# Expert weights of a routed layer loaded in 8 KB runs per partition, and the product that brings slots back to tokens taken one column half after the other

## The chip, the core and the metric

The kernel runs on one core of one Trainium2 chip. The metric is the time of one execution on the device in microseconds (us); lower is better. The core has a matrix engine (PE, with its weight loads listed as PEld), three engines for elementwise work (DVE, ACT, POOL), a queue engine (SP) that only issues transfers here, and 16 DMA engines that move the data.

## The reference, cut to what matters

256 tokens of width 1024 pass through a first block (a gated recurrence, an attention with differences, then a layer of 32 experts) and through a second block of two layers. All numbers are 32-bit. The part that the change touches is the layer of experts:

```python
x = x + hier_moe(h2, w_rg, b_rg, w_re, b_re, w_eg, w_eu, w_ed)
# each token goes to 2 of the 32 experts (one of 4 groups, two of the 8 experts in it);
# expert e on a token h of width 1024:
#   y = (silu(h @ w_eg[e]) * (h @ w_eu[e])) @ w_ed[e]
# w_eg[e], w_eu[e]: [1024, 512]; w_ed[e]: [512, 1024]; the two y are weighted by the router's gates
```

The 96 matrices are 2 MB each, 201 MB in all, and each is read once.

## The kernel before, in words

Every weight of the kernel is read from HBM as a *chunk* of 1 MB, in the order in which PE will want it. `add` (L161) enters a chunk in that list, and `pump` (L175) issues its DMA on the SP queue as soon as one of the buffers is free. SP takes the list strictly in order. A buffer comes free through `drop` when the matmuls that read it have run. During the layer of experts there is more room than elsewhere: `raw` (3 buffers) and `rawB` (4) hold a chunk each; up to four more chunks lie in the pairs `wh` and `wl` (half a chunk in each of the two, so two DMAs of 512 KB), one lies in the two `gain` tiles (two DMAs again), and single tiles that nothing else needs then (`XH`, `hT`, at the start also `XL`, `S2`/`S`, `xg`, `w`) hold one each. That makes about 14 MB.

`moe_chunks` (L1120) enters 192 chunks: for each pair of experts, first four for `w_eg`, four for `w_eu`, then four for `w_ed` (an expert's matrix is two chunks, `hf` 0 and 1). A chunk of `w_eg` or `w_eu` is a tile of 128 partitions x 4 x 512: partition p holds the rows hf * 512 + k * 128 + p for k = 0 to 3, which are 4 separate pieces of 2 KB in HBM. A chunk of `w_ed` is 128 x 2 x 1024, two pieces of 4 KB on each partition.

`moe` (L1136) first splits the normalised tokens `w` into a rounded part `xh` and a rest `xl` (ACT and DVE), picks the experts (some 25 small DVE instructions), and gives each expert 64 slots. The selection matrix `S` (tokens x slots) is built by comparing. Then 16 pairs of experts follow one another:

- every second pair, PE gathers the tokens of four experts: `xg` = (`xh` + `xl`)^T `S`, k by k (128 of the 1024 columns of the tokens at a time), and ACT copies each result to the tile `xg`;
- PE multiplies `xg` with the chunks of `w_eg` and of `w_eu`. Matmuls of 32-bit numbers are recorded in two halves; the two experts of a pair stand side by side in PE (64 columns each) and run together;
- ACT takes silu of the first product, DVE multiplies it with the second into `hid`, PE transposes `hid` in four pieces, and ACT copies them to `hidT`;
- PE multiplies `hidT` with the chunks of `w_ed` into two accumulators, one for each half of the 1024 columns;
- `split_out` scales each half by the gates and splits it into `yh` (ACT) and `yl` (DVE), in the tile `yhl`;
- PE adds `ST`^T (`yh` + `yl`) to four accumulators `po[t][n]` (`acc` in the profile): token tile t (two of 128 tokens) by column half n. That is the product from slots back to tokens.

The sum over rows k of a matmul doesn't depend on which 128 rows stand together, as long as both operands have the same rows at the same place.

All engine work is recorded through one helper line (L125), and the instruction order is the order of the code (no scheduler).

Of the kernel before, what the change touches and what calls it, by code (L numbers as in the profile page):

```python
# [10 lines left out]
F32 = mybir.dt.float32  # L11
# [8 lines left out]
T = 256  # L20
NT = 2
# [62 lines left out]
class Parts:  # L84
    """a [128, k, n] operand kept in tiles of four k each"""
# [15 lines left out]
class Counted:  # L101
    """an engine whose instructions add their estimated time (us) to a count of the work handed to it"""
# [37 lines left out]
class Kern:  # L140
# [19 lines left out]
    # ---------------------------------------------------------------- weights  # L160
    def add(self, key, src, shape, dense=True):  # L161
        """one chunk of weights: a [128, k, f] load; a dense one is split into units of half its size"""
        i = len(self.chunks)
        k, f = shape
        if not dense:
            parts = None
        elif f <= 256:
            parts = [(0, k, c, min(f, c + 128)) for c in range(0, f, 128)]
        else:
            parts = [(c, c + k // 2, 0, f) for c in (0, k // 2)]  # L170
        self.chunks.append((key, src, shape, parts))
        for n, q in enumerate(parts or ()):
            self.units.append((i, q, n == len(parts) - 1))
# [78 lines left out]
    def get(self, ahead=True):  # L252
        """next unit of the dense stream, (high part, low part)"""
        u = self.n_unit
        self.n_unit += 1
        self.split_to(u)
        if ahead:
            self.ahead(u)
        return self.hl.pop(u)

    def ahead(self, u=None):
        """split what has room: a unit with a place of its own, or a free pair of buffers"""
        self.live = [n for n in self.live if n >= (self.n_unit if u is None else u)]
        while self.n_split != self.limit and (self.n_split in self.place or len(self.live) < self.HL):
            n = self.n_split
            self.split_to(n)
            if self.n_split == n:
                break

    def own(self, pool, tag, width=2048):  # L270
        """a place for both parts of a unit in a tile that nothing else needs by then"""
        def f():
            t = pool.tile([128, width], F32R, name="own", tag=tag, bufs=1)
            return t[:, :1024], t[:, 1024:2048]
        return f

    def expect(self, key):
        """the unit that comes next belongs to this chunk"""
        i = self.units[self.n_unit][0]
        assert self.chunks[i][0] == key, (self.chunks[i][0], key)  # L280
        return sum(1 for n in range(2) if self.n_unit + n < len(self.units) and self.units[self.n_unit + n][0] == i)
# [10 lines left out]
    # ---------------------------------------------------------------- helpers  # L292
# [6 lines left out]
    def wstat(self, key, xT, ps, first=False):  # L299
        """ps columns [j * 256, ...) = (unit j of the chunk)^T xT"""  # L300
        H, L = xT
        nc = self.nc
        for j in range(self.expect(key)):
            hv, lv = self.get()
            m = hv.shape[2]
            o = ps[:m, j * T:(j + 1) * T]
            if first and j == 0:
                for w, x in ((hv, H), (lv, H), (hv, L)):
                    for k in range(KD):
                        nc.tensor.matmul(o, w[:, k], x[:, k], start=(w is hv and x is H and k == 0),  # L310
                                         stop=(x is L and k == KD - 1))
                continue
            for k in range(KD):
                nc.tensor.matmul(o, hv[:, k], H[:, k], start=(k == 0), stop=False)
                nc.tensor.matmul(o, hv[:, k], L[:, k], start=False, stop=False)
                nc.tensor.matmul(o, lv[:, k], H[:, k], start=False, stop=(k == KD - 1))
                if self.fine and k == 3:
                    self.bg()
            self.bg()

    def xstat(self, key, nu, xT, k0, pst, start, stop):
        """pst[t][half] += xT[:, k0 + k]^T (rows k of the next units)"""
# [18 lines left out]
    def xstat_all(self, keys, xT, k0s, po, first=True, tail=3, head=0):  # L341
        """rows of the chunks (two units of one row block each) into po; the last units go token tile by token tile"""
# [24 lines left out]
    def head_units(self, key):  # L367
        """the first 512 columns (of two chunks) against one token tile at a time"""
# [32 lines left out]
    def square(self, out, src):  # L401
        """sum of the squares over 1024"""
# [3 lines left out]
    def msq_end(self, ss):  # L406
        """(mean square + eps) ** -0.5, [128, 1]"""
# [16 lines left out]
    def boundary(self, w, po, gpost, gpre, HL=None, F=None, src=None, r2=None, head=None, rest=None, then=None):  # L424
        """x += po (through gpost * rmsnorm), then w = gpre * rmsnorm(x) and its transpose, split or plain"""
# [156 lines left out]
    def gain(self, ap, scale=1.0, eng=None):  # L582
        """a vector of 1024 on every partition"""
# [6 lines left out]
    def load_vecs(self, pool, items, name):  # L590
        """vectors of 128*n elements as rows, then (vec_cols) as columns [128, n] of one tile"""
# [16 lines left out]
    # ---------------------------------------------------------------- block 1  # L608
# [9 lines left out]
    def block1(self):  # L618
# [43 lines left out]
        # ---- c: convolution and silu (twice its value is kept)  # L662
# [36 lines left out]
        # ---- relative bias: rows over the distance, then one shifted row per query  # L699
# [10 lines left out]
        # ---- lambda  # L710
# [58 lines left out]
    def mlstm(self, wmq, wmk):  # L769
# [20 lines left out]
        # ---- gates, their running sums and maxima  # L790
# [7 lines left out]
        # rows of v (with a column of ones)  # L798
# [16 lines left out]
        # running over both chunks: u and M relative to the start cancel where they are used  # L815
        # stacked rows: u at 0, M_in - M at 64, -m at 96
# [14 lines left out]
        # running maxima on every partition  # L831
# [11 lines left out]
        # weight of each key for the state: exp(u - M_end)  # L843
# [196 lines left out]
    def toeplitz_load(self, hk, bd, h0, step):  # L1040
        """hk[p, h, k] = bd[h0 + step * h, p + k] for four rows h"""
# [4 lines left out]
    def toeplitz_mm(self, hk, J, dst, scale=1.0):  # L1046
        """dst[q] = hk[127 - q]"""
# [17 lines left out]
    def band_bias(self, p):  # L1065
        """attention bias of block 2 with its mask, heads in the order (key head, half of the pair, pair)"""
# [19 lines left out]
    def softplus_steps(self, scr, x, n, sign):  # L1086
        """log(1 + exp(sign * x)) on the first n partitions, in steps; the last one yields it"""
# [3 lines left out]
        def lag(n):  # L1091
            """each step waits for the one before"""
            self.load["dve"] += LAG * n
# [25 lines left out]
    # ---------------------------------------------------------------- mixture of experts  # L1119
    def moe_chunks(self):  # L1120
        eg, eu, ed = self.a["w_eg"], self.a["w_eu"], self.a["w_ed"]
# [3 lines left out]
        for p in range(16):  # L1125
            for nm, w in (("eg", eg), ("eu", eu)):
                for hf in range(2):
                    for e in (2 * p, 2 * p + 1):
                        self.add((nm, e, hf), w[0, e, hf * 512:(hf + 1) * 512].rearrange("(k p) f -> p k f", p=128),
                                 (4, 512), False)  # L1130
            for hf in range(2):
                for e in (2 * p, 2 * p + 1):
                    self.add(("ed", e, hf), ed[0, e, hf * 256:(hf + 1) * 256].rearrange("(k p) f -> p k f", p=128),
                             (2, 1024), False)

    def moe(self):  # L1136
# [11 lines left out]
        # ---- router  # L1148
        for t in range(NT):
            nc.scalar.activation(xh[:, t], self.w[:, t], AF.Copy)  # L1150
        nc.vector.tensor_sub(xl[:, 0], self.w[:, 0], xh[:, 0].bitcast(F32))
# [7 lines left out]
        def first_max(src, n, nm):  # L1159
            """value of the maximum and a one-hot of its first place"""  # L1160
# [28 lines left out]
        # ---- place of each token in its experts' lists (1, 2, ...; 0: not of that expert)  # L1189
# [4 lines left out]
        nc.vector.tensor_sub(xl[:, 1], self.w[:, 1], xh[:, 1].bitcast(F32))  # L1194
# [17 lines left out]
        # ---- gates  # L1212
# [38 lines left out]
        for pr in range(16):  # L1251
# [30 lines left out]
            # slots back to tokens, and the gate of each slot  # L1282
# [9 lines left out]
            nc.scalar.activation(hid[:2 * CAP], gu[0][:2 * CAP], AF.Silu)  # L1292
            nc.vector.tensor_mul(hid[:2 * CAP], gu[1][:2 * CAP], hid[:2 * CAP])
# [27 lines left out]
            for t in range(NT):  # L1321
                for m, y in enumerate((yh, yl)):
                    for n in range(2):
# [11 lines left out]
    def overflow(self, gov, flag):  # L1335
        """tokens beyond an expert's slots: every expert on all tokens, weighted by their gates"""
# [39 lines left out]
    # ---------------------------------------------------------------- block 2  # L1376
# [104 lines left out]
    def load_layer(self, l):  # L1481
        """per-channel and per-head parameters of one layer"""
# [38 lines left out]
    def mix(self, l):  # L1521
# [27 lines left out]
        # ---- dt  # L1549
# [5 lines left out]
        # ---- convolution channels  # L1555
# [18 lines left out]
        # ---- attention inputs  # L1574
# [18 lines left out]
        # ---- z and rg through silu (twice its value)  # L1593
# [11 lines left out]
        # ---- retention inputs  # L1605
# [19 lines left out]
        # ---- gates and branches  # L1625
# [50 lines left out]
    def bg(self, force=False):  # L1676
        """work that runs beside the projections: as much as the vector and scalar engines have time for"""
# [30 lines left out]
    def ssd(self):  # L1708
        """plain yield: go on after the next unit of weights; yield 1: go on if there is time"""
# [16 lines left out]
        # running sums: one column per head, and rows for every partition  # L1726
# [105 lines left out]
        # ---- gate and norm  # L1832
# [208 lines left out]
    def block2(self):  # L2041
# [4 lines left out]
        with self.tc.tile_pool(name="fin", bufs=1) as p:  # L2046
# [5 lines left out]
            # x becomes x * gain: the norm's scale comes after, and the next norm's from the scaled squares  # L2052
# [8 lines left out]
            def scale(t):  # L2061
                """r1 = (m + eps) ** -0.5, r1 * r2 = (m2 + eps * (m + eps)) ** -0.5 with m2 of x * gain"""
# [129 lines left out]
```

## Time and profile before

| what | value |
|---|---|
| median of three runs | 2200.3 us |
| the three runs | 2200.3, 2207.75, 2188.7 us |
| span of the profiled execution | 2188.1 us |
| PE busy, share of the span | 2094.6 us, 96% |
| DVE, ACT busy | 1107.7 us (51%), 916.0 us (42%) |
| moved by DMA | 500.05 MB, mean 229 GB/s |

A profile shows one execution. A busy PE need not be at its peak, since the ends of matmuls are modelled: in a run of matmuls that follow one another without a gap each is shown longer than its share. The page cuts the span into 40 slices of 54.7 us; for each it gives the busy share of every engine in tenths, and the bytes moved. A row of the windows view gives for one stretch the busy time of each engine, then the clock that PE was granted (1.00 is full), the mean busy share of the 16 DMA engines (it can pass 1, as one packet of an engine overlaps the next) and the GB/s moved. In a timeline row stand start, duration, engine, operation with its tiles, how many such instructions were merged, and in brackets how long the engine had been idle before and what ended that. SPq rows are DMA issues; such a row lasts as long as SP was held by it.

### The profile page before, as it was taken

What the parts mean: (1) busy time and instruction counts of PE and PEld (TensorE: products, weight loads), DVE (VectorE), ACT (ScalarE), POOL (GpSimd) and SP (SyncE); (2) the same over time, 40 slices, a digit from 0 to 9 for tenths busy, and PEclk for the clock granted to TensorE, in tenths of its full rate; (3) what the DMA queues carried; (4) which work ended last, traced back from release to release, by engine and by line L of the source; (5) the groups of instructions that cost most, each with busy time, mean ns of one, the idle gap of its engine ahead of it and who ended that gap; (6) DMA issues with size and microseconds to landing.
All of it is one profiled execution on the core that took longest, in us unless ns stands there. A gap on an engine that the chain in (4) does not pass through costs nothing. (4 is left out here: it accounts for less than half of the span.)

```text
span 2188.1 us, 33683 instructions
## 1 busy us (share of the span) xinstructions
PE 2094.6 (96%) x14031; PEld 1701.1 (78%) x14031; DVE 1107.7 (51%) x1778; ACT 916.0 (42%) x1420; POOL 95.4 (4%) x137
## 2 busy tenths in 40 slices
PE   8979999998897999999999999999999999999998
PEld 7854334333335998999999899889989999997996
DVE  5852011001004655777575655555558775756554
ACT  4441111111014554555644454444446555445442
POOL 3010000000002100000000000010000000001000
PEclk9989999999999999999999999999999999999999
DMA  8389999999997865556247475556546463555652
GB/s 250 122 298 332 375 394 392 396 393 394 397 393 192 227 214 167 168 186 220 89 134 233 145 232 183 193 192 194 194 137 226 137 212 102 167 185 187 218 194 76
DMA packets 316059, 500.05 MB, mean 229 GB/s; under 512 B 11868, under 2 KB 208940, under 8 KB 315392
## 3 DMA queue, kind: packets, MB, share of 16 engines
q1 hardware_dynamic: 309088, 474.88, 63.2%
q0 software_dynamic: 6816, 22.99, 3.6%
q8 instruction: 112, 1.84, 0.3%
q14 instruction: 43, 0.35, 0.0%
HBM read 494.62 MB, written 3.21 MB: 228 GB/s over the span
## 5 line engine op out<-in xcount | busy, mean ns | idle before, releaser
L125 PE MATMUL mm<-xTH,wh 128*128 128x256 f32 x2416 | 679.9, 281 | 0.0
L125 PE MATMUL mm<-xTH,wl 128*128 128x256 f32 x2416 | 672.3, 278 | 3.3 <-DVE wl L125 3.3
L125 PE MATMUL mm<-xTL,wh 128*128 128x256 f32 x2416 | 671.5, 278 | 0.0
L125 DVE TENSOR_TENSOR wl<-raw,wh 128x1024 fp32r<-128x1024 f32 (+1 forms) x380 | 460.2, 1218 | 265.8 <-ACT wh L125 263.8
L125 ACT ACTIVATE wh<-raw 128x1024 fp32r<-128x1024 f32 (+1 forms) x380 | 396.3, 1051 | 212.7 <-PE mm L125 140.1
L125 PEld LDWEIGHTS mm<-xTH,wh 128*128 128x128 f32 x2416 | 454.0, 188 | 6.9 <-issue 5.0
L125 PEld LDWEIGHTS mm<-xTH,wl 128*128 128x128 f32 x2416 | 453.2, 188 | 4.9 <-DVE wl L125 4.3
L125 PEld LDWEIGHTS mm<-xTL,wh 128*128 128x128 f32 x2416 | 452.9, 187 | 2.1 <-issue 1.0
L125 DVE TENSOR_TENSOR hid<-mm,hid 128x512 f32<-128x512 f32 x16 | 11.1, 692 | 289.3 <-PE mm L125 289.3
L125 DVE TENSOR_TENSOR wl<-fraw,wh 128x1024 fp32r<-128x1024 f32 x92 | 112.2, 1225 | 81.7 <-ACT wh L125 81.0
L125 ACT ACTIVATE wh<-fraw 128x1024 fp32r<-128x1024 f32 x92 | 97.1, 1057 | 91.2 <-PE mm L125 48.6
L125 PE MATMUL acc<-wh,fhH 128*128 128x512 f32 x304 | 99.9, 397 | 0.0
L125 PE MATMUL acc<-wh,fhL 128*128 128x512 f32 x304 | 99.7, 396 | 0.0
L125 PE MATMUL acc<-wl,fhH 128*128 128x512 f32 x304 | 99.7, 396 | 0.0
L125 DVE SCALAR_TENSOR_TENSOR yhl<-mm,gs,yhl 128x512 fp32r<-128x512 f32 x32 | 24.0, 751 | 138.4 <-ACT yhl L125 137.3
L125 PE MATMUL mm<-rawB,xg 128*64 128x512 f32 x304 | 82.8, 599 | 2.2 <-DMA rawB<-in_w_eu_dram 2.1
L125 PE MATMUL mm<-raw,xg 128*64 128x512 f32 x264 | 77.6, 597 | 5.0 <-DMA raw<-in_w_eu_dram 4.8
L125 PE MATMUL mm<-yyH,wh 128*128 128x256 f32 x256 | 73.3, 286 | 0.0
L125 PE MATMUL mm<-yyL,wh 128*128 128x256 f32 x256 | 72.1, 282 | 0.0
L125 PE MATMUL mm<-yyH,wl 128*128 128x256 f32 x256 | 72.1, 282 | 0.0
L125 ACT ACTIVATE hidT<-mm 128x512 f32<-128x512 f32 x16 | 9.6, 597 | 146.6 <-PE mm L125 146.6
L125 ACT ACTIVATE yhl<-mm,gs 128x512 fp32r<-128x512 f32 x32 | 22.0, 687 | 115.8 <-PE mm L125 113.8
(532 smaller groups left out, 3326.3 us busy)
## 6 DMA issues: line engine op xcount, KB each, us to landing
raw<-in_w_in_dram SPq DMA_DIRECT2D x88, 1024.0 KB, 5.2
raw<-in_w_ffn_in_dram SPq DMA_DIRECT2D x52, 1024.0 KB, 5.7
fraw<-in_w_ffn_in_dram SPq DMA_DIRECT2D x28, 1024.0 KB, 7.1
raw<-in_w_ffn_out_dram SPq DMA_DIRECT2D x24, 1024.0 KB, 4.9
rawB<-in_w_eg_dram SPq DMA_DIRECT2D x23, 1024.0 KB, 14.6
rawB<-in_w_ed_dram SPq DMA_DIRECT2D x22, 1024.0 KB, 13.8
raw<-in_w_branch_dram SPq DMA_DIRECT2D x22, 1024.0 KB, 5.4
fraw<-in_w_ffn_out_dram SPq DMA_DIRECT2D x20, 1024.0 KB, 5.0
```

What stands on the lines that cost most here:

```text
L125: return f(out, *args, **kw)
```

## The change

Three things change, all in `moe_chunks` and `moe`.

1. The rows of a chunk are chosen otherwise. Partition p now holds rows p * 8 + hf * 4 + k (k = 0 to 3) of `w_eg` and `w_eu`, and rows p * 4 + hf * 2 + k (k = 0, 1) of `w_ed`. In HBM these are 8 KB in one piece, and the pieces of neighbouring partitions lie 16 KB apart.
2. The other operands are put in the same order: the split of the tokens reads `w` with a step of 8 numbers and writes `xh` and `xl` as before, and the two instructions that make `hid` read the two products in PSUM with a step of 4 numbers.
3. The loops of the product from slots to tokens are turned: column half n outermost, then the rounded part and the rest, then the token tile.

```diff
-                        self.add((nm, e, hf), w[0, e, hf * 512:(hf + 1) * 512].rearrange("(k p) f -> p k f", p=128),
+                        self.add((nm, e, hf), w[0, e].rearrange("(p k) f -> p k f", k=KD)[:, hf * 4:hf * 4 + 4],
                                  (4, 512), False)
             for hf in range(2):
                 for e in (2 * p, 2 * p + 1):
-                    self.add(("ed", e, hf), ed[0, e, hf * 256:(hf + 1) * 256].rearrange("(k p) f -> p k f", p=128),
+                    self.add(("ed", e, hf), ed[0, e].rearrange("(p k) f -> p k f", k=4)[:, hf * 2:hf * 2 + 2],
                              (2, 1024), False)
...
+        wp_ = [self.w[:, t].rearrange("q (p k) -> q k p", k=KD) for t in range(NT)]
+        xhp, xlp = ([x[:, t].rearrange("q (k p) -> q k p", k=KD) for t in range(NT)] for x in (xh, xl))
         for t in range(NT):
-            nc.scalar.activation(xh[:, t], self.w[:, t], AF.Copy)
-        nc.vector.tensor_sub(xl[:, 0], self.w[:, 0], xh[:, 0].bitcast(F32))
+            nc.scalar.activation(xhp[t], wp_[t], AF.Copy)
+        nc.vector.tensor_sub(xlp[0], wp_[0], xhp[0].bitcast(F32))
...
-        nc.vector.tensor_sub(xl[:, 1], self.w[:, 1], xh[:, 1].bitcast(F32))
+        nc.vector.tensor_sub(xlp[1], wp_[1], xhp[1].bitcast(F32))
...
-            nc.scalar.activation(hid[:2 * CAP], gu[0][:2 * CAP], AF.Silu)
-            nc.vector.tensor_mul(hid[:2 * CAP], gu[1][:2 * CAP], hid[:2 * CAP])
+            hp = hid[:2 * CAP].rearrange("s (k p) -> s k p", k=4)
+            gp_ = [g[:2 * CAP].rearrange("s (p k) -> s k p", k=4) for g in gu]
+            nc.scalar.activation(hp, gp_[0], AF.Silu)
+            nc.vector.tensor_mul(hp, gp_[1], hp)
...
-            for t in range(NT):
+            for n in range(2):
                 for m, y in enumerate((yh, yl)):
-                    for n in range(2):
+                    for t in range(NT):
                         nc.tensor.matmul(po[t][n], ST[:2 * CAP, t * 128:(t + 1) * 128], y[:2 * CAP, n],
```

The rest of the diff is comments.

On SP the order of the loads stays, and so do their buffers; their shapes change. Here are the first loads of expert weights (the last number is the shape of the tile on the SBUF side: partitions, then the pieces). Before:

```order
L207 DMA rawB<-in_w_eg_dram 128x4x512 x4
L207 DMA XL<-in_w_eu_dram 128x4x512
L207 DMA XH<-in_w_eu_dram 128x4x512
L207 DMA raw<-in_w_eu_dram 128x4x512 x2
L207 DMA raw<-in_w_ed_dram 128x2x1024
L201 DMA wh<-in_w_ed_dram 128x1024
L201 DMA wl<-in_w_ed_dram 128x1024
```

and of the change:

```order
L207 DMA rawB<-in_w_eg_dram 128x2048 x4
L207 DMA XL<-in_w_eu_dram 128x2048
L207 DMA XH<-in_w_eu_dram 128x2048
L207 DMA raw<-in_w_eu_dram 128x2048 x2
L207 DMA raw<-in_w_ed_dram 128x2048
L201 DMA wh<-in_w_ed_dram 128x1024
L201 DMA wl<-in_w_ed_dram 128x1024
```

Nothing moved; a whole chunk is now one piece of 2048 numbers (8 KB) on each partition, while a half in `wh` or `wl` has a piece of 4 KB: that is as before for `w_ed`, and twice as long as before for `w_eg` and `w_eu`.

On PE one place of each pair is in another order, the product from slots to tokens. In this pair acc_1611 and acc_1612 are the two column halves of the first token tile, acc_1613 and acc_1614 those of the second. Before:

```order
L125 MATMUL acc_1611<-yhl_2644,ST_2595 128x512
L125 MATMUL acc_1612<-yhl_2644,ST_2595 128x512
L125 MATMUL acc_1611<-yhl_2644,ST_2595 128x512
L125 MATMUL acc_1612<-yhl_2644,ST_2595 128x512
L125 MATMUL acc_1613<-yhl_2644,ST_2595 128x512
L125 MATMUL acc_1614<-yhl_2644,ST_2595 128x512
L125 MATMUL acc_1613<-yhl_2644,ST_2595 128x512
L125 MATMUL acc_1614<-yhl_2644,ST_2595 128x512
```

and of the change:

```order
L125 MATMUL acc_1611<-yhl_2644,ST_2595 128x512
L125 MATMUL acc_1613<-yhl_2644,ST_2595 128x512
L125 MATMUL acc_1611<-yhl_2644,ST_2595 128x512
L125 MATMUL acc_1613<-yhl_2644,ST_2595 128x512
L125 MATMUL acc_1612<-yhl_2644,ST_2595 128x512
L125 MATMUL acc_1614<-yhl_2644,ST_2595 128x512
L125 MATMUL acc_1612<-yhl_2644,ST_2595 128x512
L125 MATMUL acc_1614<-yhl_2644,ST_2595 128x512
```

Of each group of four, the first two read `yh` of a half and the next two its `yl`. Before, the second matmul needed `yh` of the second half; now that is the fifth.

## Rows read from the trace of the kernel before

**Rows 1.** The page, 40 slices: PE busy in tenths, GB/s moved.
```profile
PE   8979999998897999999999999999999999999998
...
GB/s 250 122 298 332 375 394 392 396 393 394 397 393 192 227 214 167 168 186 220 89 134 233 145 232 183 193 192 194 194 137 226 137 212 102 167 185 187 218 194 76
```

**Rows 2.** Windows: the stage of the experts (clock, DMA share, GB/s last).
```profile
200.00:232.00 32.00, 30.34 (x144) 12.65 (x140) 7.68 (x10) 5.00 (x9) 0.00 (x0) 1.00 1.00 367
232.00:656.00 424.00, 391.48 (x1772) 158.53 (x1771) 36.57 (x79) 58.78 (x115) 6.79 (x11) 1.00 1.04 393
```

**Rows 3.** Windows inside that stage.
```profile
300.00:318.00 18.00, 16.75 (x80) 6.37 (x77) 2.75 (x6) 1.97 (x3) 0.00 (x0) 1.00 1.05 387
318.00:330.00 12.00, 12.00 (x57) 4.02 (x58) 0.00 (x0) 0.60 (x1) 0.00 (x0) 1.00 1.03 405
...
322.00:324.00 2.00, 2.00 (x12) 0.58 (x9) 0.00 (x0) 0.00 (x0) 0.00 (x0) 1.00 1.03 412
```

**Rows 4.** Timeline of SP (DMA issues), 300 to 322 us.
```profile
300.35 9.40 SPq L207 DMA_DIRECT2D raw<-in_w_eu_dram  x3
309.85 2.53 SPq L201 DMA_DIRECT2D wh<-in_w_ed_dram  x1
```

**Rows 5.** Timeline of ACT: the copy to hidT, once in each pair.
```profile
193.24 0.60 ACT L125 ACTIVATE hidT<-mm 128x512 f32<-128x512 f32 x1 [8.01 <-PE mm L125]
...
249.85 0.60 ACT L125 ACTIVATE hidT<-mm 128x512 f32<-128x512 f32 x1 [7.78 <-PE mm L125]
...
333.48 0.60 ACT L125 ACTIVATE hidT<-mm 128x512 f32<-128x512 f32 x1 [7.78 <-PE mm L125]
...
658.66 0.60 ACT L125 ACTIVATE hidT<-mm 128x512 f32<-128x512 f32 x1 [11.74 <-PE mm L125]
```

**Rows 6.** DMA issues: tile, source, count, KB each, median us to landing.
```profile
wh<-in_w_eu_dram SPq DMA_DIRECT2D x17, 512.0 KB, 11.9
...
wh<-in_w_ed_dram SPq DMA_DIRECT2D x16, 512.0 KB, 12.0
...
wh<-in_w_eg_dram SPq DMA_DIRECT2D x11, 512.0 KB, 11.8
...
acsB<-acsd POOLq DMA_DIRECT2D x4, 1024.0 KB, 9.0
...
gain<-in_w_eg_dram SPq DMA_DIRECT2D x6, 512.0 KB, 10.4
```

**Rows 7.** The page: packets by size, and the queues of the program's own code.
```profile
DMA packets 316059, 500.05 MB, mean 229 GB/s; under 512 B 11868, under 2 KB 208940, under 8 KB 315392
...
q8 instruction: 112, 1.84, 0.3%
q14 instruction: 43, 0.35, 0.0%
```

**Rows 8.** Timelines of PE and PEld in one pair (306 to 318 us).
```profile
306.56 0.66 PE L125 MATMUL mm<-c,hid 128*128 128x128 f32 x4 [0.18 <-DVE hid L125]
...
314.96 0.51 PE L125 MATMUL acc<-yhl,ST 128*128 128x512 f32 x1
315.80 2.22 PE L125 MATMUL acc<-yhl,ST 128*128 128x512 f32 x7 [0.33 <-ACT yhl L125]
...
316.59 0.99 PEld L125 LDWEIGHTS acc<-yhl,ST 128*128 128x128 f32 x5 [0.49 <-DVE yhl L125]
```

**Rows 9.** DVE by line and form (count, busy us, mean ns).
```profile
L125 DVE TENSOR_TENSOR hid<-mm,hid 128x512 f32<-128x512 f32 x16 | 11.1, 692 | 289.3 <-PE mm L125 289.3
...
L125 DVE TENSOR_TENSOR xl<-w,xh 128x1024 fp32r<-128x1024 f32 x2 | 2.4, 1222 | 2.4 <-ACT xh L125 2.4
...
L125 DVE TENSOR_REDUCE les<-lem 128x16 f32<-128x64 f32 x1 | 0.3, 265 | 0.0
```

**Rows 10.** Timeline of DVE at the end of the router.
```profile
164.46 1.22 DVE L125 TENSOR_TENSOR xl<-w,xh 128x1024 fp32r<-128x1024 f32 x1
...
166.19 0.23 DVE L125 SCALAR_TENSOR_TENSOR pos<-mm,mk 128x64 f32<-128x64 f32 x1 [0.51 <-PE mm L125]
```

## The prediction

> **What bounds the kernel now.** I read the page's slices first. PE stands at 9 tenths nearly everywhere, but in slices 5 to 12 (219 to 656 us) the GB/s row stands at 375 to 397, against 76 to 245 in every slice behind them [rows 1]: the stage of the experts is the one place where the DMA engines are full. The windows of the stage say so too: from 232 to 656 us they moved 393 GB/s at a busy share of 1.04, while PE shows 391.5 busy of 424 us [rows 2]. Both look full, so the pace of the pairs has to tell which one waits.
>
> The copy to hidT marks the same place of each pair [rows 5]. From 193.24 to 249.85 us two pairs took 56.6 us; the first five intervals, up to 333.48, fit that pace. From 333.48 to 658.66 ten pairs took 325.2 us. At the first pace they would take 5 x 56.6 = 283 us, and four small products for a later bias lie among them, some 1.7 us each, so 290. PE thus lost about 35 us in the second part, with the DMA engines full throughout. The buffers explain the two parts: two pairs need 24 chunks, 25.17 MB, in 56.6 us, which is 445 GB/s. At 393 the stream falls behind by 52 GB/s from the start; the chunks loaded ahead cover that for some 150 us, and then every chunk comes late. So DMA sets the end of this stage, and PE could be at most about 35 us earlier.
>
> The rate within the stage depends on the rows that are moved. From 300 to 318 us, with `w_eg` and `w_eu` (2 KB pieces) on the queues, it was 387. From 318 to 330 it was 405, in its best 2 us 412 [rows 3]. SP began to issue `w_ed` (4 KB pieces) at 309.85 [rows 4], and such loads land 12 us after their issue [rows 6], which is that stretch.
>
> **1. The longer pieces.** The time of one piece on one of 16 engines is 16 x bytes / rate: 16 x 2048 / 387 = 84.7 ns; 16 x 4096 / 405 to 412 = 161.8 to 159.1 ns. The window at 405 has some 2 KB pieces at its edges and the one at 412 is a peak, so I take 409, 160.2 ns. A straight line through both gives 8 KB in 160.2 + 2 x 75.5 = 311 ns, so 421 GB/s. How many pieces grow? 17 + 16 + 11 = 44 chunks go in halves through `wh`/`wl` [rows 6] and 9 through `gain` (its row for `w_eg` has 6 halves, `w_eu` and `w_ed` as many), 53 of 192. The other 139 get 8 KB, the halves have 4 KB. The mean rate is 1 / (0.724 / 421 + 0.276 / 409) = 418. The 424 us of the window at 393 shrink by 424 x (1 - 393 / 418) = **25 us**. With 405 for 4 KB the same working gives 412 and 20 us; with 412 it gives 422 and 29 us. If 8 KB is no faster than 4 KB the mean is 409 and the gain 17 us; nothing in the trace excludes a gain of zero (below); at the top stand PE's 35 us.
>
> Are there pieces of 8 KB at all? The page counts 316059 - 315392 = 667 packets of 8 KB or more, of which the code's queues have 112 + 43 [rows 7]. The other 512 are four loads of 128 rows of 8 KB into `acsB` [rows 6], on POOL's queue. So such rows go out as one packet there. On SP's queue no load of before has them.
>
> The Trainium skill, "DMA: Bandwidth & Descriptors", section on why small descriptors are slow, gives a fixed 3 cycles per packet beside one cycle per 32 bytes. By that, 4 KB would be 2.3% faster than 2 KB; the rows show 4.7 to 6.5%. By the page's ratio the whole change would be worth about 2.4% of the stage, an estimate of 10 us; the rows say 25, and I go by the rows.
>
> **2. The head of the stage.** From 200 to 232 us the rate was 367, not 393 [rows 2]: PE frees buffers there only just in time, and SP, strictly in order, waits for them. At 418 the stream falls behind PE's 445 by 27 instead of 52, so this phase lasts about twice as long: 32 us more at 26 of 393 less, **-2 us** of the gain. Between zero and twice that.
>
> **3. Steps in DVE's and ACT's reading.** The trace has one read of single numbers with a step: the reduce `les<-lem`, 64 numbers in 265 ns [rows 9]. From `hid` (512 in 692) and `xl` (1024 in 1222) a number costs 1.035 ns and an instruction 162, so 64 would take 228; the step costs about 0.6 ns a number.
> - The two `xl`: 0.6 us each. The second starts at 164.46 for 1.22 us, and `pos` behind it started at 166.19 after waiting 0.51 for PE [rows 10]: 164.46 + 1.22 + 0.6 = 166.3, so 0.1 us late, and all pairs with it. Doubled instructions, with ACT's `xh` too, would cost about 1.7. I take **0.1 us**.
> - `hid`: 512 numbers read from PSUM, where no row shows a step. Below: nothing. Above: doubled, 0.7 us. By the reduce 0.3 us, taken. It stands on PE's path, which waits 0.18 for it already [rows 8]: 16 x 0.3 = 5 us if PE were the bound. What hides it is PE's later wait for weights, some 12 us of 35 left after part 1; without that cover 5, at most 11 us. I take 0. The silu before it has the whole product with `w_eu` to hide in.
>
> The Trainium skill, "Vector Engine (DVE) Microarchitecture Reference", section on the SBUF access granule, says that a port loses about 0.65 cycle on each number that isn't beside its neighbour, more for small steps. The reduce agrees (0.6 ns); for PSUM no run here shows it.
>
> **4. The turned product.** In the pair at 314.96 us the first matmul ran, the second began at 315.80 (`yh` of the second half), the fourth waited for DVE until 316.59, and four more of some 0.22 us followed [rows 8]. Now only the first four need the first half; the second half's `yl`, ready at 316.59 as before, is wanted by the seventh. One matmul and not four lies behind it, so PE is done 3 x 0.22 = 0.65 us sooner, 10 us over 16 pairs if PE were the bound. It isn't: PE then waits that much longer for the next chunk. I take 0; with part 3 it raises what PE could save from 35 to about 40 us. At the end of the last pair it gains nothing that I can name, since the additions behind it run one after the other on DVE.
>
> **Sum**: -25 + 2 + 0.1 = -23 us. The profiled execution goes from 2188.1 to 2165. Its span is as short as the fastest of the three runs (2188.7 to 2207.75), so against the median I predict 2200.3 - 23 = **2177 us**, 1.05% less. Runs of one kernel spread by 19 us here; a measurement can tell about 1% from no change.
>
> **Rivals.**
> - **The gain per packet ends at 4 KB** (the engines cut pieces there, or the line bends). Then 409 GB/s, 17 us less part 2: about 2185. For it: no load of before shows 8 KB on SP's queue; the page's 10 us also lies here, 2191. Against: the 512 packets. Chance 0.20.
> - **The stream overtakes PE.** At 428 GB/s or more 35 us are gone and PE is the bound; then parts 3 and 4 count too, 5 back and 10 off: 2160 to 2165. For it: a peak of 412 with 4 KB puts 8 KB at 426. Against: the halves keep 28% at 4 KB. Chance 0.08.
> - **Nothing**: the 393 is set by something that both lengths share, and part 1 is empty. Against: 387 and 405 side by side in one stage. About 2200. Chance 0.08.
> - **Slower, by the step in HBM.** Before, a load reads 1 MB in one run; now 128 pieces 16 KB apart, and the engines read addresses that differ by powers of two. Should these fall on the same part of the memory, the rate sinks. At 393 the gain is zero, at 374 the stage takes 424 x (393 / 374 - 1) = 22 us more, 2222; below that it is slower by over 1%. No row has such a load, so nothing excludes it, and nothing speaks for it either. Chance 0.07. The Trainium skill, "DMA: Bandwidth & Descriptors", measured facts (HBM row pitch), lists 207 GB/s at a pitch of 512 KB against 214 in full, and much less from 2 MB up; at that ratio the estimate would be 380 GB/s, 2215. Its pitches are 32 times as large, and no run here shows them.
>
> **How the numbers follow.** The forecast has 0.57. Its own bounds, 20 and 29 less 2, give 2173 to 2182, which straddles 1%: slightly over half of it falls beyond. With the overtaking stream and a little of the first rival, faster by over 1% has 0.47; slower by over 1% has 0.06; within 1% the rest, 0.47. The range takes in the first rival, the overtaking stream's near end and the spread of the runs, and leaves out most of the last two: 2155 to 2197.
>
> **What would show it.** Right: the count of packets under 2 KB stays near 208940, and some 17800 packets (139 x 128) of 8 KB appear; windows of the stage at 410 to 420 GB/s; the last copy to hidT near 636 instead of 658.66; `hid` near 1.0 us, `xl` near 1.8; the acc matmuls of a pair with one wait instead of two. Everything behind the stage merely moves up. Wrong in part 1: windows still at 387 to 409. Wrong in the bound: 415 or more, but intervals between hidT copies that stay over 30 us in the mean of odd and even pairs with PE waiting for DVE or ACT. Wrong in part 3: `hid` over 1.4 us, and early pairs longer than 28.3 us in the mean.

## The result and the profile after

| kernel | median | runs | ratio to before (95% interval) |
|---|---|---|---|
| before | 2201.36 us | 2188.7 to 2207.75 (4) | |
| the change | 2173.73 us | 2172.28 to 2177.87 (4) | 0.9889 (0.9861 to 0.9917) |

The change makes the kernel about 1.1% faster; predicted were 2177 us and 1.05%. Two more comparisons on other chips are among the experiments, with ratios of 0.9903 and 0.9899.

In the page of the changed kernel the 40 slices show where it happened: slices 6 to 11 stand at 414 to 420 GB/s, where they stood at 392 to 397 before [rows 1]. The packets moved as well: there were 667 of 8 KB or more [rows 7], now there are 265499 - 247040 = 18459, which is 139 x 128 = 17792 more, and none changed below 2 KB.

```profile
GB/s 252 117 281 322 384 414 416 415 416 417 420 384 186 183 221 158 197 159 213 98 144 225 136 252 194 194 193 178 191 143 208 146 212 108 156 194 183 214 195 76
DMA packets 265499, 500.05 MB, mean 230 GB/s; under 512 B 11868, under 2 KB 208940, under 8 KB 247040
```

Windows of the changed kernel, in the stage of the experts; the columns are those of [rows 2], with the GB/s last. The first row is the head of the stage, the second nearly the whole of the rest:

```profile
200.00:232.00 32.00, 31.08 (x145) 11.23 (x142) 6.40 (x9) 3.38 (x6) 0.00 (x0) 1.00 0.97 372
...
232.00:640.00 408.00, 385.02 (x1803) 162.24 (x1802) 38.46 (x83) 60.44 (x118) 6.79 (x11) 1.00 1.02 415
```

It is 415 where [rows 2] has 393; 418 was predicted. The copies to hidT, from the timeline of ACT (start, duration, operation), mark the stage's length:

```profile
198.47 0.60 ACT L125 ACTIVATE hidT<-mm 128x512 f32<-128x512 f32 x1 [8.01 <-PE mm L125]
...
253.85 0.60 ACT L125 ACTIVATE hidT<-mm 128x512 f32<-128x512 f32 x1 [7.78 <-PE mm L125]
...
640.66 0.60 ACT L125 ACTIVATE hidT<-mm 128x512 f32<-128x512 f32 x1 [10.85 <-PE mm L125]
```

From the first to the last it takes 640.66 - 198.47 = 442.2 us; before it took 658.66 - 193.24 = 465.4 [rows 5]. That is **23.2 us less**, and the sum of the prediction was 25 - 2 = 23. "Stage" below is this distance, read from the one profile of each kernel in the same way. The three profiles of the change give 442.2, 442.2 and 443.5 us, so a difference of 1 or 2 us between two stages shows nothing by itself.

### The profile page after: what moved, and what is told of

It is laid out like the page before. It is cut to its first block, busy times and chain, and to the rows that moved or that the text cites. A ratio compares the mean times of both kernels' runs of the same rounds, so it can differ in the third digit from the quotient of the medians.

```text
span 2176.1 us, 33683 instructions
## 1 busy us (share of the span) xinstructions
PE 2089.0 (96%) x14031; PEld 1710.5 (79%) x14031; DVE 1109.1 (51%) x1778; ACT 918.2 (42%) x1420; POOL 95.1 (4%) x137
## 2 busy tenths in 40 slices
DMA packets 265499, 500.05 MB, mean 230 GB/s; under 512 B 11868, under 2 KB 208940, under 8 KB 247040
## 5 line engine op out<-in xcount | busy, mean ns | idle before, releaser
L125 PEld LDWEIGHTS acc<-wh,fhL 128*128 128x128 f32 x304 | 57.3, 188 | 13.9
## 6 DMA issues: line engine op xcount, KB each, us to landing
rawB<-in_w_eg_dram SPq DMA_DIRECT2D x23, 1024.0 KB, 13.8
```

Of the source, the lines that this page charges most:

```text
L125: return f(out, *args, **kw)
```

## The experiments

The theory: the loads bind the stage, a piece of n bytes costs an engine a fixed part of some 9 ns and 37.75 ns for each KB, and the rest of the change is hidden. The rivals: PE binds as much as the loads; it is the new rows and not the length; the gain ends at 4 KB.

All ratios are to the kernel before on the same chip.

| run | median | ratio (95% interval) | stage | GB/s, 350 to 630 us |
|---|---|---|---|---|
| before | | | 465.4 | 395 |
| e1, the change | 2175.83 | 0.9903 (0.9879 to 0.9926) | 442.2 | 417 |
| e2, old product order | 2172.32 | 0.9900 (0.9875 to 0.9925) | 443.7 | 417 |
| e3, product order alone | 2192.10 | 0.9987 (0.9970 to 1.0005) | 464.2 | 395 |
| e4, before with less PE | 2191.31 | 0.9986 (0.9971 to 1.0002) | 463.2 | 395 |
| e5, new rows, short pieces | 2195.23 | 0.9996 (0.9978 to 1.0015) | 463.1 | 394 |
| e6, all pieces 4 KB | 2179.27 | 0.9929 (0.9903 to 0.9955) | 449.2 | 409 |
| e7, `w_eg`, `w_eu` alone | 2177.35 | 0.9905 (0.9871 to 0.9938) | 444.4 | 414 |
| e8, pieces of 1 KB | 2231.03 | 1.0161 (1.0126 to 1.0195) | 495.7 | 368 |
| e9, the change | 2175.22 | 0.9899 (0.9882 to 0.9917) | 443.5 | 417 |
| e10, `wh` and `wl` one tile | 2168.77 | 0.9872 (0.9851 to 0.9893) | 440.0 | 420 |
| e11, the change with less PE | 2172.25 | 0.9893 (0.9873 to 0.9914) | 440.2 | 418 |
| e12, `w_ed` alone | 2195.21 | 0.9995 (0.9976 to 1.0015) | 462.3 | 398 |

### Which part of the change it is

**The whole change again.**

> The whole change again, against the kernel before. Theory (the stage of the experts is bound by its loads, longer pieces are loaded faster, the rest is hidden): from the first copy to hidT to the last 442 us as in the first profile of the change (465 before), 415 GB/s there, 20 to 28 us less in all. Rival (the 28 us between the first two medians are partly luck of TensorE's clock in other places): the stage shrinks by 23 us all the same, but the total by 10 to 18.

The ratio is 0.9903, 20 us between the medians, and the stage is 442.2 us: theory. e9 below says the same.

**Without the turned product.**

```diff
-            for n in range(2):
+            for t in range(NT):
                 for m, y in enumerate((yh, yl)):
-                    for t in range(NT):
+                    for n in range(2):
                         nc.tensor.matmul(po[t][n], ...
```

> The change with the product from slots to tokens in its old order. Theory (loads set the end): within 3 us of the whole change, stage 442 to 445 us, though PE's pace in early pairs goes back up by 0.65 us a pair (two early pairs 56.6 instead of 55.4 us). Rival (the turned product brings part of the gain): 7 to 10 us slower than the whole change.

Its ratio is that of the whole change, and its stage is 1.5 us longer. Its median lies 3.5 us below that of e1, half a us outside what was expected and not on the rival's side. PE's early pace is back at 56.6 us for two pairs, as the timeline of ACT shows (252.36 - 195.75):

```profile
195.75 0.60 ACT L125 ACTIVATE hidT<-mm 128x512 f32<-128x512 f32 x1 [8.01 <-PE mm L125]
...
252.36 0.60 ACT L125 ACTIVATE hidT<-mm 128x512 f32<-128x512 f32 x1 [7.78 <-PE mm L125]
```

So the turned product does what it should to PE, 0.6 us a pair, and the total doesn't show it.

**The turned product alone**, the last hunk of the diff put on the kernel before.

> The kernel before with only the product from slots to tokens turned. Theory: as before within 3 us; early pairs 1.2 us shorter per two, but the later ones longer by as much, since the loads stay at 393 GB/s; stage 464 to 466 us. Rival (PE is the bound as much as the loads): 10 us faster, stage 455.

No difference that can be measured: the median is 4.0 us lower, 1 us outside what was expected, and the interval takes in 1. The stage is 464.2 us. Two early pairs take 55.4 us, and the later ones give it back: the last copy to hidT comes at 662.01, 464.2 after the first.

```profile
197.82 0.60 ACT L125 ACTIVATE hidT<-mm 128x512 f32<-128x512 f32 x1 [8.01 <-PE mm L125]
...
253.18 0.60 ACT L125 ACTIVATE hidT<-mm 128x512 f32<-128x512 f32 x1 [7.78 <-PE mm L125]
...
662.01 0.60 ACT L125 ACTIVATE hidT<-mm 128x512 f32<-128x512 f32 x1 [11.75 <-PE mm L125]
```

### Do the loads bind, or PE?

**The kernel before with less work for PE.**

```diff
-                            for n, (t, src) in enumerate((t, src) for t in range(NT) for src in (xh, xl)):
+                            for n, (t, src) in enumerate((t, src) for t in range(NT) for src in (xh,)):
...
-                for m, y in enumerate((yh, yl)):
+                for m, y in enumerate((yh,)):
```

> The kernel before with less work for PE in the stage: the gather takes only the rounded part of the tokens (its sums lack the rest) and the product from slots to tokens only the rounded part of y; that is some 1.8 us of matmuls and a wait of 0.6 us less in each pair, 30 to 38 us over 16 pairs. Theory (loads set the end): total within 5 us of before, stage 460 to 465 us, at 393 GB/s, with longer waits of PE for loads. Rival (PE is the bound): 30 us or more faster.

PE did less: in this kernel's window it is busy for 237.5 of 280 us, while before it was 256.0. The rate did not move. First the kernel with less work, then the kernel before:

```profile
350.00:630.00 280.00, 237.48 (x1010) 89.58 (x1006) 23.57 (x52) 34.52 (x71) 4.18 (x7) 1.00 1.04 395
```

```profile
350.00:630.00 280.00, 256.03 (x1146) 104.56 (x1144) 23.52 (x52) 38.82 (x76) 4.19 (x7) 0.99 1.04 395
```

The stage came out 2.2 us shorter and the total the same within the interval. By the first two pairs (52.5 us instead of 56.6) PE needs 2.1 us less for each, 33 us over 16 pairs; the later pairs gave it back as waiting. Its waits for loads from 333 to 660 us add up to 38.8 us, where they were 16.5 before (who waited for whom, us in total, times, longest). First the kernel with less work, then the kernel before:

```profile
PE mm L125 <- DMA rawB<-in_w_eu_dram: 10.2, 7, 1.9
PE mm L125 <- DMA raw<-in_w_eu_dram: 8.9, 5, 2.3
...
PE mm L125 <- DMA hT<-in_w_eu_dram: 4.6, 3, 3.0
```

```profile
PE mm L125 <- DMA raw<-in_w_eu_dram: 4.8, 3, 1.6
...
PE mm L125 <- DMA rawB<-in_w_eu_dram: 2.1, 2, 1.6
```

**The change with the same work left out.**

> The whole change with less work for PE, as in the run of the kernel before with less (no rest of the tokens in the gather, no rest of y in the product): some 30 us less matmuls over 16 pairs. Theory (the loads still bind the change): total within 4 us of the change, stage 437 to 441 us. Rival (after the change PE binds as much as the loads): 10 us or more under the change, stage 432 or less.

The loads bind the changed kernel too: the stage is 440.2 us against 443.5 in e9 on the same chip, though PE needs 1.7 us less for an early pair (52.0 for two, not 55.4), 27 us over 16 pairs. PE is now nearer to its own limit, though: the pairs it could run at 55.4 us for two would need about 5 x 55.4 + 7 = 284 us for the ten last intervals, which took 640.66 - 335.65 = 305 in the profile of the change. Some 21 us are left where there were 35 by the same working.

### Is it the length of the pieces?

**New rows, short pieces.** Every second row of a chunk has a load of its own, so that nothing lies in one piece; the order of the operands is that of the change.

```diff
-                if len(src.shape) == 3:
+                if parts is None:
+                    for n in range(2):
+                        self.nc.sync.dma_start(v[:, n::2], src[:, n::2])
+                elif len(src.shape) == 3:
                     self.nc.sync.dma_start(v, src)
```

(The halves in `wh`, `wl` and `gain` are loaded row by row in the same way. `parts is None` picks the chunks of the experts.)

> The whole change, but every load of expert weights cut in two so that no piece is longer than before: a chunk of w_eg or w_eu in pieces of 2 KB, one of w_ed in pieces of 4 KB, at the new rows. Theory (the length of the piece is what counts): 393 GB/s as before, stage 464 us as with the turned product alone, total 2190 to 2198. Rival (the new rows, or fewer waits, bring the gain and not the length): stage 442 to 450, total 2172 to 2182. Other rival (the 16 KB step costs something that the longer pieces hide): under 385 GB/s, stage over 473.

All of the gain is gone: 394 GB/s, stage 463.1 us, ratio 0.9996. The new addresses, 16 KB apart, neither bring anything nor cost anything that shows. With the change's own rate that settles two rivals, the slower one with the step in HBM among them:

```profile
350.00:630.00 280.00, 254.16 (x1140) 104.42 (x1140) 23.55 (x52) 38.80 (x76) 4.18 (x7) 1.00 1.04 394
```

**All pieces 4 KB.** Two loads for each chunk, each with half of the partition's 8 KB:

```diff
-                if len(src.shape) == 3:
+                if parts is None:
+                    for n in range(2):
+                        self.nc.sync.dma_start(v[:, n * (k // 2):(n + 1) * (k // 2)], src[:, n * (k // 2):(n + 1) * (k // 2)])
+                elif len(src.shape) == 3:
                     self.nc.sync.dma_start(v, src)
```

> The whole change, but every chunk loaded by two loads, each with one piece of 4 KB on a partition: all pieces 4 KB. Theory (a fixed part of some 9 ns in each packet, on a straight line): 405 to 409 GB/s, stage 447 to 451 us, total 5 to 9 us over the whole change, about 2181. Rival (the gain ends at 4 KB): 415 GB/s and the time of the whole change. Other rival (twice as many loads cost time on SP): under 400 GB/s.

It has 409 GB/s, the number that the prediction took between 405 and 412, and a stage 6 to 7 us longer than the change:

```profile
350.00:630.00 280.00, 261.69 (x1192) 105.88 (x1190) 24.95 (x54) 40.24 (x79) 4.47 (x8) 1.00 1.03 409
```

So the gain doesn't end at 4 KB: about 16 of the 23 us come from there, the last 7 from 8 KB. By the medians alone the two could not be told apart for certain, since their intervals overlap; the rates (409 and 417) and the stages tell them apart. That twice as many loads cost nothing that shows is seen as well, as the rate is the one worked out from the lengths.

**Pieces of 1 KB**, the other way along the same line:

```diff
+                if parts is None and f == 512:
+                    for n in range(2):
+                        self.nc.sync.dma_start(v[:, :, n * 256:(n + 1) * 256], src[:, :, n * 256:(n + 1) * 256])
...
```

(The halves are cut in the same way.)

> The kernel before with each load of w_eg and w_eu cut by columns, in pieces of 1 KB; w_ed as before. Theory (straight line: 84.7 - 37.75 = 47 ns for 1 KB, 349 GB/s for these, 367 in the mean): 424 x (393 / 367 - 1) = 30 us more in the stage, 493 to 498 us, total 2220 to 2230. Rival (the step from 387 to 405 GB/s has another cause than a fixed part per piece): within 8 us of before.

The stage is 30.3 us longer than before, and the time 1 us over the upper end of what was expected. In a stretch with only these loads in flight the rate is 348 GB/s; 349 was worked out. In the same run, whose pieces of `w_ed` are 4 KB, the best windows of 6 us have 410 or 411, and none reaches the rate of 8 KB:

```profile
350.00:630.00 280.00, 242.06 (x1032) 97.37 (x1033) 20.79 (x46) 34.30 (x67) 5.45 (x9) 0.98 1.07 368
452.00:468.00 16.00, 13.68 (x56) 5.58 (x55) 1.50 (x2) 1.94 (x3) 0.00 (x0) 1.00 1.10 348
```

The same kind of stretch in the changed kernel, from 480 to 498 us with whole chunks in flight, completes the line (e9 has 422 there too):

```profile
480.00:498.00 18.00, 16.78 (x76) 6.34 (x73) 2.75 (x6) 1.98 (x3) 0.00 (x0) 1.00 1.02 422
```

| piece | GB/s | 16 x bytes / rate | more than the row above |
|---|---|---|---|
| 1 KB, e8, 452 to 468 us | 348 | 47.1 ns | |
| 2 KB, before [rows 3] | 387 | 84.7 ns | 37.6 for 1 KB |
| 4 KB, e6, 350 to 630 us | 409 | 160.2 ns | 75.5 for 2 KB |
| 8 KB, the change, 480 to 498 us | 422 | 310.6 ns | 150.4 for 4 KB |

Each KB costs 37.6 to 37.8 ns, and some 9 ns are left over in each piece. That the piece has such a part is shown by the four lengths; what an engine spends it on was not tried.

**Which matrices.** e7 takes `w_ed` back to its old rows, e12 takes `w_eg` and `w_eu` back, each with the order of the operand that goes with them.

> The whole change, but w_ed as before (4 KB pieces) and hid in its old order. Theory: mean 413 to 415 GB/s, stage 443 to 446 us, 2 to 4 us over the whole change. Rival (w_ed counts as much for each byte as the others): stage 450, a third of the gain gone, 7 us over it.

> The whole change, but w_eg and w_eu as before (2 KB and their old rows): only w_ed in 8 KB, and the turned product. Theory: mean 396 to 397 GB/s, 3 us less in the stage than the turned product alone: 460 to 462 us, total within 1% of before.

`w_eg` and `w_eu` alone have a stage of 444.4 us, `w_ed` alone 462.3 with the turned product in it (464.2 without `w_ed`). So `w_ed`, a third of the bytes, brings some 2 us of the 23, no more than single profiles differ by; the rates say it more surely, 398 against 395 in e3 and 414 against 417. e12 lies 0.3 us over the expected stage, and no difference of its time can be measured. This is as the line has it: in 8 KB of `w_ed` one of two pieces is saved, in 8 KB of `w_eg` or `w_eu` three of four, and of these there are twice as many bytes.

### A version that goes on

**The change again, beside one tile for `wh` and `wl`.**

> The whole change once more, as the measure for the run with one tile on the same chip: 20 to 25 us under before, stage 442 us, 415 GB/s.

```diff
-                h = self.wp.tile([128, 1024], F32R, name="wh", tag="wh", bufs=self.HL)[:]
-                l = self.wp.tile([128, 1024], F32R, name="wl", tag="wl", bufs=self.HL)[:]
+                hl = self.wp.tile([128, 2048], F32R, name="whl", tag="whl", bufs=self.HL)
+                h, l = hl[:, :1024], hl[:, 1024:]
...
+            if tag == "rawC":
+                t = pool.tile([128, 2048], F32R, name="whl", tag="whl", bufs=bufs)
+                v = t[:].bitcast(F32).rearrange("p (k f) -> p k f", k=k)
+                self.nc.sync.dma_start(v, src)
...
```

> The whole change, and wh and wl one tile of 2048 numbers, so that the 44 chunks that went in two halves go in one load with pieces of 8 KB; only 9 chunks keep 4 KB. Theory (length of the piece): mean 1 / (0.953 / 421 + 0.047 / 409) = 420 GB/s where the loads bind, against 418 by the same working: stage 1 to 3 us shorter, 439 to 441, total 1 to 3 us under the change. Rival (a buffer that comes free only as a whole starves the loads): stage 445 or more.

The stage is 440.0 us against 443.5 in e9 (442.2 in the two other profiles of the change), and the rate is what was worked out; the change has 417 in all three. First this kernel, then the change:

```profile
350.00:630.00 280.00, 264.59 (x1222) 111.30 (x1220) 24.93 (x54) 40.81 (x79) 4.24 (x8) 1.00 1.01 420
```

```profile
350.00:630.00 280.00, 262.71 (x1216) 110.39 (x1212) 24.87 (x54) 40.82 (x79) 4.31 (x8) 1.00 1.02 417
```

The median is 6.4 us under that of the change on the same chip, more than the 3.5 of the stage; the intervals (0.9851 to 0.9893 and 0.9882 to 0.9917) overlap a little. It is clearly faster than the kernel before. That its loads run faster than those of the change is shown by the rate; that the whole is faster is only likely.

## Why the prediction was right, point by point

**What bounds the stage: right.** e4 and e11 take some 30 us from PE and move the stage by 2 to 3 us; e5, e6 and e8 change the length of the pieces (and double the number of loads, which by e5 and e6 costs nothing that shows), and the stage follows from 449 to 496 us, beside 442 for the change. The 35 us that the prediction took from the pace of the pairs are not all seen as waits: the trace books 16.5 us of waits for loads there, and PE shows 296 us busy over the last ten pairs, where twice the 134 us of the first five and the later bias make 275. How the missing time divides between the two is open.

**Part 1, 25 us for the longer pieces: right**, and the straight line from 2 and 4 KB held at both ends. The mean came out at 415 from 232 to 640 us and 417 from 350 to 630, where 418 was worked out. The choice of 409 between 405 and 412 was confirmed by e6. The Trainium skill, "DMA: Bandwidth & Descriptors", section on why small descriptors are slow, has 3 cycles as the fixed part; the rows of four lengths show about 9 ns, and by the page's share the whole change would have been the 10 us that the prediction gave beside its own sum. The measurement decides for the rows.

**Part 2, the head: about right in size, but not by a phase of twice the length.** From 200 to 232 us the rate was 372, and from 232 to 280 it was 399, against 416 behind that. But the kernel before is under its full rate in the same two windows, with 367 [rows 2] and 381 against 394. First the kernel before, then the change:

```profile
232.00:280.00 48.00, 45.87 (x220) 17.67 (x220) 4.54 (x11) 5.78 (x12) 1.29 (x2) 1.00 1.03 381
280.00:400.00 120.00, 114.91 (x542) 46.72 (x540) 11.04 (x24) 17.51 (x34) 1.31 (x2) 1.00 1.04 394
```

```profile
232.00:280.00 48.00, 46.84 (x230) 19.92 (x229) 5.76 (x13) 6.81 (x14) 1.29 (x2) 1.00 1.00 399
280.00:400.00 120.00, 115.63 (x556) 47.55 (x556) 11.04 (x25) 18.25 (x36) 1.31 (x2) 1.00 1.02 416
```

Counted against its own full rate, the kernel before loses 2.2 + 1.6 = 3.8 us in the two windows and the change 3.4 + 2.0 = 5.4. The difference is 1.6 us (2.3 with the 364 and 396 against 415 of e9), where 2 was taken. The 32 us more at a low rate are not there: the last window of 8 us under 350 GB/s is 232 to 240 before (326) and 240 to 248 in the change (343). The head costs more mainly because the rate that it falls short of is higher. That 2 came out so near is in part luck.

**Part 3, reading with a step: small, as said, but both prices were mis-sized and one instruction was left out.** DVE by line and form, after the change:

```profile
L125 DVE TENSOR_TENSOR hid<-mm,hid 128x512 f32<-128x512 f32 x16 | 11.1, 692 | 270.8 <-PE mm L125 270.8
...
L125 DVE TENSOR_TENSOR xl<-w,xh 128x1024 fp32r<-128x1024 f32 x2 | 4.1, 2052 | 4.1 <-ACT xh L125 4.1
```

`hid` still takes 692 ns [rows 9]: its step in PSUM costs nothing that shows, where 0.3 us had been put down and then counted as hidden. `xl` takes 2052 ns and not the 1800 expected, 0.81 ns more for each number where 0.6 had been read from the reduce. The Trainium skill, "Vector Engine (DVE) Microarchitecture Reference", section on the SBUF access granule, has this sign and about this size for SBUF (0.65 cycle a number, more for small steps); the PSUM side is the runs' own.

The second `xl` makes PE wait 1.06 us for `S` before its first gather, and the timeline of PE has the row:

```profile
172.91 0.55 PE L125 MATMUL mm<-S,xh 128*128 128x256 f32 x1 [1.06 <-DVE S L125]
```

Before, that wait was 0.87 us, so it is 0.2 us for the predicted 0.1. The first `xl` had no price, and it has one where the router's matmuls on PE end early enough. In e9 they end at 157.22 + 4.26 = 161.48 us, but `lr`, which takes their result, stands on DVE behind the first `xl` and starts at 161.96:

```profile
157.22 4.26 PE L125 MATMUL mm<-wr,hT 128*128 128x36 f32 x32
```

```profile
160.00 2.05 DVE L125 TENSOR_TENSOR xl<-w,xh 128x1024 fp32r<-128x1024 f32 x1 [3.38 <-ACT xh L125]
161.96 0.23 DVE L125 TENSOR_TENSOR lr<-mm,br 128x72 f32<-128x72 f32 x1
```

By the timelines of PE it is 7.19 us from the end of these matmuls to the first gather in all five profiles that split the tokens in the old order. In the new order it is 7.36 to 7.39 us where the matmuls take 6.88 us, and 7.81 to 7.93 where they take 4.12 to 4.26. So part 3 costs 0.2 or 0.6 to 0.7 us, and 0.1 was in the sum.

**Part 4, the turned product: right.** PE shows the eight matmuls in one row, without the wait in their midst that [rows 8] has (and without the one that was expected to stay), and two early pairs take 1.2 us less; the total doesn't move (e2, e3).

```profile
317.74 2.44 PE L125 MATMUL acc<-yhl,ST 128*128 128x512 f32 x8
```

**Not foreseen: where the last copy to hidT would stand.** 636 us was named, it came at 640.66, although the stage was as short as predicted: it began 5.2 us later. The router's 32 matmuls began 3.1 us later, before the first engine instruction that the change touches; they took 2.6 us longer; `S` came 0.2 us later, and 0.7 us were gained behind it. The timeline of PE has the matmuls in 4.27 us before and in 6.88 after, and a window over just these matmuls has the granted clock (third number from the end):

```profile
155.56 4.27 PE L125 MATMUL mm<-wr,hT 128*128 128x36 f32 x32
```

```profile
155.56:159.83 4.27, 4.27 (x34) 4.13 (x32) 1.23 (x1) 2.62 (x4) 0.03 (x1) 0.84 1.06 373
```

```profile
158.67 6.88 PE L125 MATMUL mm<-wr,hT 128*128 128x36 f32 x32
```

```profile
158.67:165.55 6.88, 6.88 (x33) 6.74 (x32) 2.09 (x1) 4.59 (x3) 0.00 (x0) 0.50 1.04 384
```

0.50 is 1.2 instead of 2.4 GHz throughout. The change does not decide it. The fourteen profiles fall into two groups: in nine the clock is 0.50 and the matmuls take 6.88 us, in five it is 0.84 to 0.87 and they take 4.12 to 4.27. Kernels that split the tokens in the old order stand in both (e3, e8 and e12 in the first, before and e4 in the second), and so do those with the new order (e2, e5 and e9 in the second, the others in the first). The row of e3:

```profile
157.47 6.88 PE L125 MATMUL mm<-wr,hT 128*128 128x36 f32 x32
```

PE's last waits ahead of these matmuls are the same before and after (1.44, 0.4 and 0.64 us, all for `w`). What starts the half clock in one execution and not in the next was not tried.

**The total: right within what the medians can tell.** The first comparison gives 28 us, the repeats 20 and 23; that the first median lies 3 us from the forecast is in part luck. The two spans of the first comparison are only 12 us apart, 2188.1 and 2176.1, and 2165 was predicted for the second: the profiled execution was the fastest of four before and the slowest of four after. Of the 11 us that the spans lack beside the stage's 23.2, 5.2 were lost ahead of the stage and the others behind it; there, for 100 us from the last copy on, the clock was 0.91, against 0.95 before and in e9. The stage, where the clock stood at 0.98 to 1.00, is the better measure.

**The rivals.** "The gain per packet ends at 4 KB" falls to e6; "nothing" falls to the change's rate, which only the length explains (e5, e6, e8); "slower, by the step in HBM" falls to e5; "the stream overtakes PE" needed 428 GB/s, and the best kernel here has 420.

## What to carry to other kernels

Where the DMA engines are full, compare the rate in stretches with pieces of different lengths: here two lengths in one trace gave the fixed part of a piece, and a line that held at lengths the trace didn't have. A matmul's contraction rows can be dealt to partitions in any order, so weights can often be laid out as one long piece per partition for the price of reordering the small operand. Before PE's order is polished in such a stage, take work away from PE and see whether the stage gets shorter.

## What the runs showed of the hardware

- **A step was free in PSUM and dear in SBUF, but the two steps were not the same.** Reading every fourth number of PSUM left DVE at 692 ns and ACT's silu at 597 ns. Reading every eighth number of SBUF took DVE from 1222 to 2052 ns and ACT from 1048 to 2096 ns, about double. Whether it is the memory or the length of the step was not tried. ACT before, then after:

```profile
L125 ACT ACTIVATE hid<-mm 128x512 f32<-128x512 f32 x16 | 9.6, 597 | 105.1 <-PE mm L125 105.1
...
L125 ACT ACTIVATE xh<-w 128x1024 fp32r<-128x1024 f32 x2 | 2.0, 1048 | 0.0
```

```profile
L125 ACT ACTIVATE hid<-mm 128x512 f32<-128x512 f32 x16 | 9.6, 597 | 99.0 <-PE mm L125 99.0
...
L125 ACT ACTIVATE xh<-w 128x1024 fp32r<-128x1024 f32 x2 | 4.1, 2096 | 0.0
```

- **Time from issue to landing says nothing on the rate here.** The chunks of `w_eu` in `raw` landed 18.6 us after their issue instead of 14.7, at 415 instead of 393 GB/s; those of `w_eg` in `rawB` landed after 13.8 instead of 14.6. At 415 GB/s a chunk of 1 MB is moved in 2.5 us, so most of these times is spent behind other loads. Why some wait longer now was not tried. Before, then after:

```profile
rawB<-in_w_eg_dram SPq DMA_DIRECT2D x23, 1024.0 KB, 14.6
...
raw<-in_w_eu_dram SPq DMA_DIRECT2D x17, 1024.0 KB, 14.7
```

```profile
rawB<-in_w_eg_dram SPq DMA_DIRECT2D x23, 1024.0 KB, 13.8
...
raw<-in_w_eu_dram SPq DMA_DIRECT2D x17, 1024.0 KB, 18.6
```
